# Token mixers in a one-core layer kernel: order of GpSimd's work, rests around small transfers, and how partial sums of a modulation are added

## The chip, the cores and the metric

One core of a Trainium2 chip runs one program: one inference step of a hybrid layer, 512 prompt frames and 64 sample frames, model width 2048, float32 in and out. The metric is the device time of that execution in microseconds (us). Of several executions the median is taken. Beside the time there is a profile of one execution: for every engine (TensorE = PE with its weight loads PEld, VectorE = DVE, ScalarE = ACT, GpSimd = POOL, and SP, which here only issues transfers) each instruction's start, duration and what ended the wait before it.

## The reference, cut to what matters

```python
mod = silu(c) @ w_ada + b_ada                       # 6 vectors of 2048 from one conditioning vector
sh1, sc1, g1, sh2, sc2, g2 = split(mod, 6)
h = rmsnorm(x, norm1) * (1 + sc1) + sh1
proj = h @ w_in                                     # 7200 columns, split between two mixers
# GLA: 4 heads, S_t = diag(a_t) S_{t-1} + k_t v_t^T, o_t = S_t^T q_t
# GDN: 8 heads; q, k, v = silu(causal_dwconv(q|k|v, 4 taps)); q, k normalised per frame;
#      S_t = a_t (I - b_t k_t k_t^T) S_{t-1} + b_t k_t v_t^T, o_t = S_t^T q_t
#      per block: sol = triangular_solve(I + lower, rhs, unit_diagonal=True)
# both: o = rmsnorm_per_head(o) * silu(gate)
x = x + g1 * (concat(o_gla, o_gdn) @ w_out)
h = rmsnorm(x, norm2) * (1 + sc2) + sh2
x = x + g2 * conv_ffn(h)                            # conv gate, w_up 2048 x 11264, w_down 5632 x 2048
y = rmsnorm(x, final_norm)
```

Prompt and sample share the weights. Final states and convolution tails are returned too.

## The kernel before

The activations lie transposed (features on partitions, 576 frames along the free axis, in two halves of 288). Every float32 weight tile is split into a rounded high part and the rest (`split`, L598 to L600: transfer on SP, high part on ACT, low part on DVE), and each product is made of three matmuls (`mm6`, L512 and L514). The program runs in this order: a head (input transposed, modulation vectors 0 and 1, the first projections); the **mixer stage** (projections, all heads, first half of the output projection, about 240 to 1260 us of the span); second half of the output projection; the up projection (L1300 to L1302); the down projection and the last norm. The change touches only the mixer stage and its helpers.

In the mixer stage the projection gemms run k-tile by k-tile, and after each k-tile (six matmuls) `tick` is called. It advances two kinds of side work that is written as Python generators:

- *jobs*, one generator for each head (`gdn`, `gla`). `job_step` goes through the list of open jobs, oldest first, until one of them does a real step. A generator that yields `WAIT` lets the next job have the same tick; `rest(n)` yields `WAIT` n times.
- *ada*: modulation vectors 2 to 5, blocks 8 to 23 of 512 columns (`ada_block`). Eight transfers of `w_ada` per block (L764), then per step one DVE instruction (L772, 128x512) that adds a weighted row into the running sum `acc[s]`, s = 0 for prompt and 1 for sample. At the end of a block the 128 partial sums of each column are added by TensorE (L778): eight products, each with a 128x128 piece of `acc` as the stationary operand and one column of ones as the moving one; `put_mod` adds the bias. `ADA_RATE` steps are made per k-tile.

A planner places the recorded instructions: each engine's order follows the order of emission as a priority, but where an instruction's inputs come late by the planner's own cost estimates, a later one may be placed ahead of it. On the chip an engine then runs its list strictly in that order. All transfers are issued from SP's list, so a transfer that must wait holds back those behind it. `_Sooner` (`self.jv`, `self.ja`) gives the jobs' DVE and ACT instructions 80 places of priority. `issue_after(x)` adds an edge: what is recorded inside it comes after x on its engine.

A GDN head runs: decay masks (`affine_select` on POOL, L181, L182), transposes of k and q with sums of squares and `rsqrt` (DVE adds EPS, L137; POOL takes the power, L138); two sets of products (L216, L222); `inverse16`, which inverts the 16x16 diagonal blocks of the triangle on POOL: write to DRAM (L340), read back with one block per partition (L345), 14 iterations of two POOL instructions (L351, L352), a copy (L354), write and read back (L355, L358), spread to full width on DVE (L362); then levels 16, 32, 64 on TensorE (from L238); then, once v is there, four blocks of recurrence (L276 to L305); `rsqrt` of the output's squares, normalisation on ACT, transposes (L144), gate, and the output's transfer `o_put`. The next head's job is open while the one before it ends.

`gdn_conv` (L907 to L925) makes the four-tap convolution of one q, k or v tile: copies from PSUM on ACT and DVE (L914, L915), four small copies on POOL (L916 to L919), one product on ACT, three on DVE, the SiLU on ACT. `put_s` sends the 64 sample frames of a tile to DRAM (L900).

Of the kernel before, what the change touches and what calls it, by code (L numbers as in the profile page):

```python
# [16 lines left out]
P = 128  # L17
D = 2048
KD = 16
TP, TS = 512, 64  # L20
# [8 lines left out]

AHEAD, JOB_AHEAD = 80, 80  # L30

JOB_RATE, ADA_RATE = 1.0, 0.65


REST_D, REST_X, REST_T, REST_N, REST_G = 8, 16, 2, 2, 3
LATE = 3
N_EARLY = 4
N_EXTRA = 24
# [57 lines left out]
class Kern:  # L96
    def __init__(self, tc, ctx, i, o):
        self.tc, self.nc, self.ctx, self.i, self.o = tc, tc.nc, ctx, i, o
        self.n = 0
        self.cp = ctx.enter_context(tc.tile_pool(name="cp", bufs=1, side="left"))  # L100
        self.pg = ctx.enter_context(tc.tile_pool(name="pg", bufs=2, space=PSUM))
        self.c = {}
        self.jv, self.ja = _Sooner(tc, tc.nc.vector), _Sooner(tc, tc.nc.scalar)

    def load_consts(self, pool, names):
        nc = self.nc
# [19 lines left out]
        return self.m(tag).rearrange("p (b t) -> p b t", b=4)  # L126

    def small(self, w):
        return self.sp.tile([P, w], F32, tag=f"s{w}", name=self.name(f"s{w}"))

    def half(self):
        return self.sp.tile([P, P], F32, tag="sq", bufs=4, name=self.name("sq"))
# [2 lines left out]
    def rsqrt(self, out, src, n, parts=P):  # L135

        self.nc.vector.tensor_scalar_add(out[:parts, :n], src[:parts, :n], EPS)  # L137
        self.nc.gpsimd.tensor_tensor(out[:parts, :n], out[:parts, :n], self.mhalf[:parts, :n], op=ALU.pow)  # L138

    def transpose4(self, src4, n=4):  # L140

# [13 lines left out]
    def gdn(self, qF, kF, x, gain, hcols, gb_src, s0, s_out, o_put, last_level):  # L155
# [10 lines left out]
        nc, c = self.nc, self.c  # L166
# [14 lines left out]
        nc.gpsimd.affine_select(du, du, pattern=[[0, 4], [1, P]], compare_op=ALU.is_ge, fill=0.0, base=0, channel_multiplier=-1)  # L181
        nc.gpsimd.affine_select(dl, dl, pattern=[[0, 4], [-1, P]], compare_op=ALU.is_gt, fill=0.0, base=0, channel_multiplier=1)  # L182
        if pair:
            nc.gpsimd.memset(du[0:64, :, 64:P], 0.0)
# [4 lines left out]
        junk = self.half()  # L189
        kps = self.transpose4(kF)  # L190
        kT = self.m4()
        for b in range(4):
# [116 lines left out]
            nc.sync.dma_start(s_out, st)  # L309

        ss, rr = self.small(8), self.small(8)
        junk = self.half()
# [8 lines left out]
        while "gate" not in x:  # L321
            yield WAIT
        V.tensor_tensor(kF, kF, x["gate"](), op=ALU.mult)
        o_put(kF)

    def rest(self, n):
# [4 lines left out]
    def inverse16(self, a):  # L331

        nc, c, G = self.nc, self.c, self.nc.gpsimd
# [10 lines left out]
        G.memset(lane[:, 0, 0:256:17], 1.0)  # L347
        for i in range(1, 15):
            rest = slice(i + 1, 16)
            sh = [32, 15 - i, i]  # L350
            G.tensor_tensor(xt[:, rest, :i], xx[:, rest, i:i + 1].to_broadcast(sh), xx[:, i:i + 1, :i].to_broadcast(sh), op=ALU.mult)  # L351
            G.tensor_tensor(xx[:, rest, :i], xx[:, rest, :i], xt[:, rest, :i], op=ALU.add)  # L352
            yield WAIT
        G.tensor_copy(xt, xx.rearrange("p i j -> p j i"))  # L354
        nc.sync.dma_start(d1.rearrange("w q f -> q w f"), lane)  # L355
        cm = self.sp.tile([P, 2, 4, 16], F32, tag="cm", bufs=1, name=self.name("cm"))
        for w in range(2):
            nc.sync.dma_start(cm[:, w], d1[w].rearrange("(b n) (i j) -> (n i) b j", b=4, i=16))  # L358
        sh = [P, 4, 8, 16]
        t, u = self.m4(), self.m4()  # L360
        for w, x in enumerate((t, u)):
            nc.vector.tensor_tensor(x.rearrange("p b (n j) -> p b n j", n=8), cm[:, w].unsqueeze(2).to_broadcast(sh),  # L362
                                    c["bd16"].rearrange("p (n j) -> p n j", n=8).unsqueeze(1).to_broadcast(sh), op=ALU.mult)
        yield from self.rest(REST_X)
        return u, t

    def gla(self, nb, qF, kF, g, x, s0, s_out, o_put):
# [103 lines left out]
        for f in range(2):  # L471
            dst = (qd, kd3)[f]
            while f"gate{f}" not in x:
                yield WAIT
            V.tensor_tensor(dst, dst, x[f"gate{f}"](), op=ALU.mult)
            o_put(f, dst)


    def tick(self):
# [266 lines left out]
    def put_mod(self, mi, k0, m):  # L746
        self.nc.vector.tensor_tensor(
            self.mod[:, mi, k0:k0 + 4], m,
            self.vec("b_ada", mi * KD + k0, 4).unsqueeze(2).to_broadcast([P, 4, 2]), op=ALU.add)

    def scale_mod(self, out, mi, norm, k0, n=4):

# [4 lines left out]
    def ada_block(self, blk, acc, raw):  # L757

        nc = self.nc
        V, T = nc.vector, nc.tensor  # L760
        acc = [a() for a in acc]
        for k0 in range(0, KD, 2):
            w = raw().rearrange("p (k n) -> p k n", k=2)
            nc.sync.dma_start(w, self.i["w_ada"][0, k0 * P:(k0 + 2) * P, blk * 512:(blk + 1) * 512]  # L764
                              .rearrange("(k p) n -> p k n", p=P))
            for k in range(2):
                for s in range(2):
                    col = self.ct[:, s, k0 + k:k0 + k + 1]
                    if k0 + k == 0:
                        V.tensor_scalar_mul(acc[s], w[:, k], col)  # L770
                    else:
                        V.scalar_tensor_tensor(acc[s], w[:, k], col, acc[s], op0=ALU.mult, op1=ALU.add)  # L772
                    yield
        yield from self.rest(4)
        pc = self.bank()
        for j in range(4):
            for s in range(2):
                T.matmul(pc[:, 2 * j + s:2 * j + s + 1], acc[s][:, j * P:(j + 1) * P], self.c["ones"][:, 0:1],  # L778
                         start=True, stop=True)
# [116 lines left out]
    def put_s(self, name, col, write):  # L896

        t = self.sp.tile([P, TS], F32, tag="ts", bufs=4, name=self.name("ts"))
        write(t)
        self.nc.sync.dma_start(self.sd[name][:, col * TS:(col + 1) * TS], t)  # L900

    def get_s(self, name, w=512):

# [4 lines left out]
    def gdn_conv(self, ps, t, dst, name, h):  # L908

        nc = self.nc  # L910
        V, A = nc.vector, nc.scalar
        cb = self.ap.tile([P, 582], F32, tag="cb", bufs=1, name=self.name("cb"))
        acc = self.ap.tile([P, 582], F32, tag="ca", bufs=1, name=self.name("ca"))
        A.activation(cb[:, 3:515].rearrange("p (h t) -> p h t", h=2), ps[:, :, :HP], AF.Copy)  # L914
        V.tensor_copy(cb[:, 518:582].rearrange("p (h t) -> p h t", h=2), ps[:, :, HP:HT])  # L915
        nc.gpsimd.tensor_copy(cb[:, 0:3], self.zero3)  # L916
        nc.gpsimd.tensor_copy(cb[:, 515:518], self.vmap["st_conv"].rearrange("p (i t) -> p t i", i=3)[:, t])
        nc.gpsimd.tensor_copy(self.cs[:, 0, :, t], cb[:, 512:515])
        nc.gpsimd.tensor_copy(self.cs[:, 1, :, t], cb[:, 579:582])  # L919
# [4 lines left out]
        A.activation(dst, acc[:, 0:512], AF.Silu)  # L924
        self.put_s(name, h, lambda s: A.activation(s, acc[:, 515:579], AF.Silu))  # L925

# [12 lines left out]
    def gdn_heads(self):  # L939
# [19 lines left out]
        def vg(h, x):  # L959
# [5 lines left out]
            self.put_s("g", h, lambda t: A.activation(self.halves(t), ps[:, :, HP:HT], AF.Silu))  # L965
            x["gate"] = lambda: b4(gt)

        xs = [qk(0)]
        for h in range(8):
            if h < 7:  # L970
# [641 lines left out]
class _Sooner:  # L1612
# [5 lines left out]
    def __getattr__(self, name):  # L1618
        f = getattr(self.engine, name)

        def g(*a, **kw):
            with self.tc.high_priority(offset=JOB_AHEAD):
                return f(*a, **kw)
        return g


class _States:


# [55 lines left out]
```

## Time and profile before

| | before |
|---|---|
| median of 3 executions | 2979.81 us (2978.62 to 2980.59) |
| profiled execution, its own time | 2981.26 us |
| its span in the profile | 2979.5 us |
| granted TensorE clock, mean | 0.98 |
| TensorE matmul busy | 2863.4 us, 96% |
| VectorE busy | 2050.0 us, 69% |
| ScalarE busy | 1179.3 us, 40% |
| GpSimd busy | 338.0 us, 11% |
| transfers | 395.55 MB, mean 133 GB/s |

An engine's busy time is the union of its instructions. The granted clock is 1.00 at full speed. A row of the timeline gives start, duration, engine, line, operation, output and inputs, shapes, the number of merged instructions, and in brackets the idle time before and what ended it. In the waits view a row gives total idle us, number of waits, longest. A row of the windows view gives the stretch, its length, each engine's busy time and number of instructions, then the granted clock, the share of the transfer engines and GB/s.

### The profile page before, as it was taken

What the parts mean: (1) busy time and instruction counts of PE and PEld (TensorE: products, weight loads), DVE (VectorE), ACT (ScalarE), POOL (GpSimd) and SP (SyncE); (2) the same over time, 40 slices, a digit from 0 to 9 for tenths busy, and PEclk for the clock granted to TensorE, in tenths of its full rate; (3) what the DMA queues carried; (4) which work ended last, traced back from release to release, by engine and by line L of the source; (5) the groups of instructions that cost most, each with busy time, mean ns of one, the idle gap of its engine ahead of it and who ended that gap; (6) DMA issues with size and microseconds to landing.
All of it is one profiled execution on the core that took longest, in us unless ns stands there. A gap on an engine that the chain in (4) does not pass through costs nothing.

```text
span 2979.5 us, 52341 instructions
## 1 busy us (share of the span) xinstructions
PE 2863.4 (96%) x21060; PEld 2772.9 (93%) x21060; DVE 2050.0 (69%) x3234; ACT 1179.3 (40%) x2015; POOL 338.0 (11%) x609
## 2 busy tenths in 40 slices
PE   6998899999899999999999999999999999999998
PEld 3688888999889998999999999999999999999997
DVE  2366766667668867557888888888888865555555
ACT  4234444444445333245444444444444421222223
POOL 0004323333120000000011111111111100000000
PEclk8999999999999999999999999999999999999999
DMA  8864544444454446643333333333333473333221
GB/s 269 285 185 121 150 143 124 128 129 144 134 159 130 137 132 194 199 140 97 106 105 111 109 103 107 111 102 105 115 105 105 133 236 101 111 101 113 84 85 66
DMA packets 535446, 395.55 MB, mean 133 GB/s; under 512 B 59657, under 2 KB 465412, under 8 KB 535204
## 3 DMA queue, kind: packets, MB, share of 16 engines
q1 hardware_dynamic: 535204, 392.21, 44.0%
q8 instruction: 166, 2.72, 0.4%
q14 instruction: 76, 0.62, 0.1%
HBM read 356.47 MB, written 35.67 MB: 132 GB/s over the span
## 4 chain that ended last, share of the span: by engine, by line
PE 71%; DVE 3%; DMA 2%; POOL 1%; issue 1%; ACT 1%; SPq 0%; ACTq 0%; DVEq 0%; POOLq 0%
PE g L512 22%; PE bank L1301 11%; PE bank L1300 11%; PE bank L1302 11%; PE g L514 11%; DVE acc L772 1%; PE bank L405 1%; PE bank L144 1%; DMA xr<-in_w_ada_dram 1%; DMA xr<-in_x_prompt_dram 1%; PE bank L778 1%; DVE wl L600 0%; POOL m L352 0%; POOL m L351 0%; POOL s L138 0%
## 5 line engine op out<-in xcount | busy, mean ns | idle before, releaser
L1301 PE MATMUL bank<-slot,wh 128*128 128x290 f32 x2464 | 736.3, 299 | 0.0
L1300 PE MATMUL bank<-slot,wh 128*128 128x290 f32 x2464 | 734.0, 298 | 0.0
L1302 PE MATMUL bank<-slot,wl 128*128 128x290 f32 x2464 | 728.2, 296 | 0.0
L512 PE MATMUL g<-slot,wh 128*128 128x288 f32 x3168 | 551.7, 295 | 0.3 <-DVE slot L1070 0.3
L512 PE MATMUL g<-hh,wh 128*128 128x288 f32 x2048 | 473.1, 310 | 0.0
L1302 PEld LDWEIGHTS bank<-slot,wl 128*128 128x128 f32 x2464 | 470.8, 191 | 0.0
L1301 PEld LDWEIGHTS bank<-slot,wh 128*128 128x128 f32 x2464 | 469.8, 191 | 0.1
L512 PEld LDWEIGHTS g<-slot,wh 128*128 128x128 f32 x3168 | 465.8, 188 | 0.7 <-DVE slot L1070 0.5
L599 ACT ACTIVATE wh<-raw 128x1024 fp32r<-128x1024 f32 x215 | 227.5, 1059 | 601.9 <-PE g L512 572.1
L1300 PEld LDWEIGHTS bank<-slot,wh 128*128 128x128 f32 x2464 | 464.2, 188 | 0.1
L512 PE MATMUL g<-hl,wh 128*128 128x288 f32 x2048 | 461.6, 304 | 0.0
L514 PE MATMUL g<-hh,wl 128*128 128x288 f32 x2048 | 459.9, 303 | 1.6 <-DVE wl L600 1.6
L1070 DVE SCALAR_TENSOR_TENSOR slot<-g,mod,slot 128x512 f32<-128x512 f32 (+1 forms) x448 | 202.1, 492 | 284.2 <-PE g L514 283.2
L772 DVE SCALAR_TENSOR_TENSOR acc<-xr,ct,acc 128x512 f32<-128x512 f32 x480 | 340.5, 752 | 26.6 <-DMA xr<-in_w_ada_dram 26.0
L512 PEld LDWEIGHTS g<-hh,wh 128*128 128x128 f32 x2048 | 336.6, 193 | 12.1 <-issue 9.8
L514 PEld LDWEIGHTS g<-hh,wl 128*128 128x128 f32 x2048 | 338.6, 193 | 8.4 <-issue 5.9
L512 PEld LDWEIGHTS g<-hl,wh 128*128 128x128 f32 x2048 | 340.4, 193 | 4.4 <-issue 3.9
L514 PE MATMUL g<-slot,wl 128*128 128x288 f32 x1584 | 342.8, 295 | 0.0
L600 DVE TENSOR_TENSOR wl<-raw,wh 128x1024 fp32r<-128x1024 f32 x215 | 262.5, 1221 | 62.4 <-ACT wh L599 61.7
L1247 ACT ACTIVATE wh<-raw 128x1024 fp32r<-128x1024 f32 x176 | 186.0, 1057 | 221.9 <-PE bank L1301 185.6
L514 PEld LDWEIGHTS g<-slot,wl 128*128 128x128 f32 x1584 | 255.3, 188 | 0.0
L1248 DVE TENSOR_TENSOR wl<-raw,wh 128x1024 fp32r<-128x1024 f32 x176 | 215.4, 1224 | 54.3 <-ACT wh L1247 54.3
(354 smaller groups left out, 3160.9 us busy)
## 6 DMA issues: line engine op xcount, KB each, us to landing
raw<-in_w_up_dram SPq DMA_DIRECT2D x176, 512.0 KB
xr<-in_w_ada_dram SPq DMA_DIRECT2D x128, 512.0 KB
raw<-in_w_in_dram SPq DMA_DIRECT2D x100, 512.0 KB
raw<-in_w_down_dram SPq DMA_DIRECT2D x88, 512.0 KB
hraw<-in_w_ada_dram SPq DMA_DIRECT2D x64, 512.0 KB
raw<-in_w_out_dram SPq DMA_DIRECT2D x32, 512.0 KB
slot<-actd SPq DMA_DIRECT2D x44, 288.0 KB
actd<-v SPq DMA_DIRECT2D x44, 256.0 KB
```

Source lines behind the costliest of these rows:

```text
L144: self.nc.tensor.transpose(ps[:, b * P:(b + 1) * P], src4[:, b], self.c["ident"])
L512: T.matmul(ps[:, h if bank is None else bank, :n], wh, x[:, h, :n], start=f, stop=False)
L514: T.matmul(ps[:, h if bank is None else bank, :n], wl, ah[:, h, :n], start=False, stop=stop)
L599: nc.scalar.activation(hi[:, :n_], raw[:, :n_], AF.Copy)
L600: nc.vector.tensor_tensor(lo[:, :n_], raw[:, :n_], hi[:, :n_].bitcast(F32), op=ALU.subtract)
L772: V.scalar_tensor_tensor(acc[s], w[:, k], col, acc[s], op0=ALU.mult, op1=ALU.add)
L1070: self.nc.vector.scalar_tensor_tensor(x1[:, :, z], ps[:, :, c], gain[:, q:q + 1], x1[:, :, z], op0=ALU.mult, op1=ALU.add)
L1247: self.nc.scalar.activation(hi, src, AF.Copy)
L1248: self.nc.vector.tensor_tensor(lo, src, hi.bitcast(F32), op=ALU.subtract)
L1300: T.matmul(ps, wh[:, j], hi, start=(c < 3 and j == 0), stop=False, skip_group_check=True)
L1301: T.matmul(ps, wh[:, j], lo, start=False, stop=False, skip_group_check=True)
L1302: T.matmul(ps, wl[:, j], hi, start=False, stop=(j == NPAIR - 1), skip_group_check=True)
```

## The change

1. `_InTurn` wraps GpSimd as `self.pool`: each of its instructions gets an edge to the one emitted before it. `rsqrt`, the masks and `inverse16` use it, so GpSimd's list is the order of emission for them.
2. `rest` is split up. The two rests of `inverse16` (8 ahead of the iterations, 16 at its end) become 2 and 3 around the first transfers, 6 ahead of the iterations, 2, 3, 4 and 4 around the second transfers and the spreading; the sum with the 14 iterations is 38 k-tiles, as before. The rest ahead of the last transposes of a GDN head goes from 2 to 4, and 4 are new ahead of `o_put`.
3. Small tiles `small(w)` have 8 buffers instead of 2; results of squares that nobody reads go to one tile `scrap` and no longer to one of the four `sq` buffers.
4. `gdn_conv`: the four POOL copies are gone. The zeros are written once, into a tile that stays; the state's columns are copied by DVE, and both output tails by one DVE copy after the convolution.
5. `put_s` issues its transfer from ACT's list (except for `ag`, which stays on SP).
6. `ada_block`: the partial sums are added with ones as the stationary operand in four products, each 32 output rows wide (row groups 0, 32, 64, 96 of one bank), 256 moving columns; ACT copies the 128x256 result, two rests, two transposes, and two `put_mod` of two columns each.
7. `ADA_RATE` goes from 0.65 to 0.72 steps per k-tile.

```diff
-JOB_RATE, ADA_RATE = 1.0, 0.65
-REST_D, REST_X, REST_T, REST_N, REST_G = 8, 16, 2, 2, 3
+JOB_RATE, ADA_RATE = 1.0, 0.72
+REST_S, REST_L, REST_D, REST_X, REST_U, REST_T, REST_N, REST_O, REST_G = 2, 3, 6, 4, 4, 2, 4, 4, 3
...
     def small(self, w):
-        return self.sp.tile([P, w], F32, tag=f"s{w}", name=self.name(f"s{w}"))
+        return self.sp.tile([P, w], F32, tag=f"s{w}", bufs=8, name=self.name(f"s{w}"))
+    def junk(self):
+        if not self.scrap:
+            self.scrap.append(self.kp.tile([P, P], F32, name="scrap"))
+        return self.scrap[0]
...
-        self.nc.gpsimd.tensor_tensor(out[:parts, :n], out[:parts, :n], self.mhalf[:parts, :n], op=ALU.pow)
+        self.pool.tensor_tensor(out[:parts, :n], out[:parts, :n], self.mhalf[:parts, :n], op=ALU.pow)
...
         V.tensor_tensor(kF, kF, x["gate"](), op=ALU.mult)
+        yield from self.rest(REST_O)
         o_put(kF)
...
+        yield from self.rest(REST_S)
         nc.sync.dma_start(d0[:P * pitch].rearrange("(p f) -> p f", p=P), a.rearrange("p b t -> p (b t)"))
+        yield from self.rest(REST_L)
...
         G.tensor_copy(xt, xx.rearrange("p i j -> p j i"))
+        yield from self.rest(REST_S)
         nc.sync.dma_start(d1.rearrange("w q f -> q w f"), lane)
+        yield from self.rest(REST_L)
...
+        yield from self.rest(REST_X)
         t, u = self.m4(), self.m4()
...
-        yield from self.rest(REST_X)
+        yield from self.rest(REST_U)
...
         yield from self.rest(4)
-        pc = self.bank()
-        for j in range(4):
-            for s in range(2):
-                T.matmul(pc[:, 2 * j + s:2 * j + s + 1], acc[s][:, j * P:(j + 1) * P], self.c["ones"][:, 0:1],
-                         start=True, stop=True)
-        self.put_mod(blk // 4, 4 * (blk % 4), pc[:, :8].rearrange("p (j s) -> p j s", s=2))
+        ps = self.bank()
+        for s in range(2):
+            for h in range(2):
+                r = 64 * s + 32 * h
+                T.matmul(ps[r:r + 32, :256], self.c["ones"][:, :32], acc[s][:, h * 256:(h + 1) * 256], start=True, stop=True)
+        rows = self.sp.tile([P, 256], F32, tag="qc", bufs=3, name=self.name("rows"))
+        self.nc.scalar.activation(rows, ps[:, :256], AF.Copy)
+        yield from self.rest(2)
+        pc = self.transpose4(rows.rearrange("p (b t) -> p b t", b=2), 2)
+        for h in range(2):
+            self.put_mod(blk // 4, 4 * (blk % 4) + 2 * h, pc.rearrange("p b (s c) -> p b s c", s=2)[:, :, :, 32 * h], 2)
...
-        self.nc.sync.dma_start(self.sd[name][:, col * TS:(col + 1) * TS], t)
+        (self.nc.sync if name == "ag" else self.nc.scalar).dma_start(self.sd[name][:, col * TS:(col + 1) * TS], t)
...
-        cb = self.ap.tile([P, 582], F32, tag="cb", bufs=1, name=self.name("cb"))
+        cb = self.conv_in
...
-        nc.gpsimd.tensor_copy(cb[:, 0:3], self.zero3)
-        nc.gpsimd.tensor_copy(cb[:, 515:518], self.vmap["st_conv"].rearrange("p (i t) -> p t i", i=3)[:, t])
-        nc.gpsimd.tensor_copy(self.cs[:, 0, :, t], cb[:, 512:515])
-        nc.gpsimd.tensor_copy(self.cs[:, 1, :, t], cb[:, 579:582])
+        V.tensor_copy(cb[:, 515:518], self.vmap["st_conv"].rearrange("p (i t) -> p t i", i=3)[:, t])
...
+        V.tensor_copy(self.cs[:, :, :, t], cb[:, 512:646].rearrange("p (s c) -> p s c", s=2)[:, :, 0:3])
...
+class _InTurn:
+    def __init__(self, tc, engine):
+        self.tc, self.engine, self.last = tc, engine, None
+    def __getattr__(self, name):
+        f = getattr(self.engine, name)
+        def g(*a, **kw):
+            with self.tc.issue_after(self.last) if self.last is not None else nullcontext():
+                r = f(*a, **kw)
+            self.last = self.tc.nc.cur_bb.bb.instructions[-1]
+            return r
+        return g
```

More of the change, by code (lines that the diff above doesn't have):

```diff
@@ L101, in __init__ @@
         self.pg = ctx.enter_context(tc.tile_pool(name="pg", bufs=2, space=PSUM))
-        self.c = {}
+        self.c, self.scrap = {}, []
         self.jv, self.ja = _Sooner(tc, tc.nc.vector), _Sooner(tc, tc.nc.scalar)
+        self.pool = _InTurn(tc, tc.nc.gpsimd)
     def load_consts(self, pool, names):
@@ L180, in gdn @@
         A.activation(du, du, AF.Exp, scale=-1.0)
-        nc.gpsimd.affine_select(du, du, pattern=[[0, 4], [1, P]], compare_op=ALU.is_ge, fill=0.0, base=0, channel_multiplier=-1)
-        nc.gpsimd.affine_select(dl, dl, pattern=[[0, 4], [-1, P]], compare_op=ALU.is_gt, fill=0.0, base=0, channel_multiplier=1)
+        self.pool.affine_select(du, du, pattern=[[0, 4], [1, P]], compare_op=ALU.is_ge, fill=0.0, base=0, channel_multiplier=-1)
+        self.pool.affine_select(dl, dl, pattern=[[0, 4], [-1, P]], compare_op=ALU.is_gt, fill=0.0, base=0, channel_multiplier=1)
         if pair:
-            nc.gpsimd.memset(du[0:64, :, 64:P], 0.0)
+            self.pool.memset(du[0:64, :, 64:P], 0.0)
         A.activation(gb, gb, AF.Exp)
         ss, kt = self.small(8), self.sp.tile([P, 4, 4], F32, tag="kt", bufs=3, name=self.name("kt"))
-        junk = self.half()
+        junk = self.junk()
         kps = self.transpose4(kF)
@@ L311, in gdn @@
         ss, rr = self.small(8), self.small(8)
-        junk = self.half()
+        junk = self.junk()
         for b in range(4):
@@ L331, in inverse16 @@
     def inverse16(self, a):
-        nc, c, G = self.nc, self.c, self.nc.gpsimd
+        nc, c, G = self.nc, self.c, self.pool
         pitch = 4 * P
@@ L475, in gla @@
             V.tensor_tensor(dst, dst, x[f"gate{f}"](), op=ALU.mult)
-            o_put(f, dst)
+        yield from self.rest(REST_O)
+        for f in range(2):
+            o_put(f, (qd, kd3)[f])
     def tick(self):
@@ L744, in sum_early, with put_mod @@
             nc.sync.dma_start(self.halves(self.sd[name][:, h * TS:(h + 1) * TS]), acc[:, :, HP:])
-    def put_mod(self, mi, k0, m):
+    def put_mod(self, mi, k0, m, n=4):
         self.nc.vector.tensor_tensor(
-            self.mod[:, mi, k0:k0 + 4], m,
-            self.vec("b_ada", mi * KD + k0, 4).unsqueeze(2).to_broadcast([P, 4, 2]), op=ALU.add)
+            self.mod[:, mi, k0:k0 + n], m,
+            self.vec("b_ada", mi * KD + k0, n).unsqueeze(2).to_broadcast([P, n, 2]), op=ALU.add)
     def scale_mod(self, out, mi, norm, k0, n=4):
@@ L966, in vg @@
             x["gate"] = lambda: b4(gt)
+        self.conv_in = self.ap.tile([P, 646], F32, name="conv_in")
+        nc.vector.tensor_copy(self.conv_in[:, 0:3], self.zero3)
         xs = [qk(0)]
```

## The prediction, made before the changed kernel was run

> **What bounds the kernel now.** I read the windows first, then the waits of PE, then the timeline around each long wait. The windows of the mixer stage (us; then PE, PEld, DVE, ACT, POOL busy, granted clock, transfer share, GB/s):
>
> ```profile
> 240.00:800.00 560.00, 508.58 (x3744) 491.73 (x3743) 360.48 (x610) 247.30 (x616) 178.67 (x359) 0.95 0.47 134
> 800.00:1150.00 350.00, 340.75 (x2480) 323.60 (x2479) 264.89 (x523) 147.64 (x310) 26.15 (x46) 0.98 0.47 138
> 1150.00:1260.00 110.00, 106.19 (x753) 101.42 (x752) 71.17 (x106) 32.87 (x54) 1.64 (x16) 0.97 0.77 219
> ```
>
> PE is the bound, with little idle: 51.4 + 9.3 + 3.8 = 64.5 us. But the clock is below 1.00 here: 0.05 x 560 + 0.02 x 350 + 0.03 x 110 = 38 us of full clock are missing. I put 8 of them into the idle time itself (an estimate), so 30 us of work are lost. All the change can give back here is about 95 us, and PE work that it removes. Where the idle time is (us, times, longest):
>
> ```profile
> PE bank L144 <- ACT m L1623: 28.1, 10, 9.1
> ...
> PE bank L276 <- DVE st L1623: 8.7, 1, 8.7
> PE bank L778 <- DVE m L1623: 8.3, 1, 8.3
> ...
> PE bank L144 <- ACT qkv L924: 5.9, 4, 1.9
> ```
>
> The first row is one place: the last transposes of each GDN head, which wait for the normalisation behind `rsqrt`. I followed the longest, around 305 to 313 us, through SP, DVE, POOL and PE:
>
> ```profile
> 293.39 0.38 SPq L598 DMA_DIRECT2D raw<-in_w_in_dram  x1
> 305.31 0.33 SPq L355 DMA_DIRECT2D d<-m  x1
> 309.62 0.75 DVE L772 SCALAR_TENSOR_TENSOR acc<-xr,ct,acc 128x512 f32<-128x512 f32 x1 [7.86 <-DMA xr<-in_w_ada_dram]
> 310.29 1.22 DVE L600 TENSOR_TENSOR wl<-raw,wh 128x1024 fp32r<-128x1024 f32 x1
> 311.43 0.16 DVE L137 TENSOR_SCALAR s<-s 128x4 f32<-128x4 f32 x1
> 304.69 0.59 POOL L354 COPY m<-m 32x256 f32<-32x256 f32 x1
> 311.67 1.44 POOL L138 TENSOR_TENSOR s<-s,mhalf 128x4 f32<-128x4 f32 x1 [6.39 <-DVE s L137]
> 313.60 0.47 PE L144 MATMUL bank<-consts,m 128*128 128x128 f32 x1 [9.14 <-ACT m L1623]
> ```
>
> Backwards: PE waited for the power, the power for DVE's add, DVE stood 7.86 us at the ada sum for a `w_ada` tile, and SP had issued nothing from 293.8 to 305.3, because L355 stood in its list ahead of its time and waited for POOL's copy: the inverse of the *next* head. Other heads have other roads to the same place:
>
> ```profile
> 376.67 0.27 DVE L137 TENSOR_SCALAR s<-s 128x4 f32<-128x4 f32 x1
> 380.18 0.59 POOL L354 COPY m<-m 32x256 f32<-32x256 f32 x1
> 380.75 1.01 POOL L138 TENSOR_TENSOR s<-s,mhalf 128x4 f32<-128x4 f32 x1
> 382.24 0.47 PE L144 MATMUL bank<-consts,m 128*128 128x128 f32 x1 [4.64 <-ACT m L1623]
> 456.21 0.69 DVE L362 TENSOR_TENSOR m<-cm,consts 128x512 f32<-128x512 f32 x1 [4.46 <-DMA cm<-d]
> 753.84 4.04 DMA xr<-in_w_ada_dram
> ```
>
> At 376.9 the add was done, but POOL finished the next head's inverse first (to 380.8). At 456 DVE stood at the spreading L362 for that inverse's transfer. The last row is from the chain of waits: ahead of the 8.7 us at L276 lies a late `w_ada` tile again. So the next head's inverse, placed too early in three lists, is one cause. And a wait costs more than itself; here PE works again since 313.6:
>
> ```profile
> 318.00:320.00 2.00, 2.00 (x11) 2.00 (x10) 2.00 (x5) 1.01 (x2) 1.27 (x2) 0.59 0.62 181
> 320.00:322.00 2.00, 2.00 (x18) 2.00 (x17) 2.00 (x4) 0.00 (x0) 0.00 (x0) 1.00 1.05 326
> ```
>
> 11 matmuls in 2 us instead of 18, until about 319.6: 6 us at half speed, 3 us lost.
>
> **The change part by part.**
>
> *GpSimd in order, and the rests.* I counted the generators in k-tiles. In the steady state head 2's iterations are emitted from k-tile 147 (now 150), after head 1's `rsqrt` at 141; the spreading moves from 161 to 173, the first level stays at 177. In the trace, though, the iterations ran before that `rsqrt`, since POOL had nothing else. With the edges they can't: SP's and DVE's long waits then fall behind the old head's end, where PE has only gemm work with weights buffered three deep. The transposes come 2 k-tiles later, 1.3 us (12 matmuls at the last row's 18 in 2 us). The chain after the last square is add, power 1.0 to 1.4, normalisation and queueing. I take 0.5 us of wait left per head: 28.1 becomes 4, a gain of 24 (ends: 10, if half the heads find DVE at another late transfer; 28). The 8.7 us at L276 have the same road, `w_ada` behind L355: gain 8.7 (ends 0 and 8.7). The 8.3 us at L778 belong to head 0, which has no head before it; only the convolution's POOL copies go from ahead of its inverse: gain 2 (ends 0 and 8.3).
>
> What it costs: the inverse starts later. For head 2:
>
> ```profile
> L347 POOL MEMSET m<- x1: 115/115/115, 365.1 to 365.1; 32x16 f32 x1
> L362 DVE TENSOR_TENSOR m<-cm,consts x2: 691/692/693, 385.4 to 387.0; 128x512 f32<-128x512 f32 x2
> L238 PE MATMUL bank<-m,m x24: 220/275/275, 410.2 to 489.1; 128*128 128x64 f32 x24
> ```
>
> It ran from 365.1 to 380.8, 15.7 us; from the copy's end to the second spreading's end at 387.7 took 6.9; the first level came at 410.2, 22.5 us of slack. Now it starts after the power, 376.9 + 1.3 = 378.2, and ends with the spreading at 378.2 + 15.7 + 6.9 = 400.8. The level comes at 410.2 less the 4.64 us of wait and about 3 us of half clock: 402.6. That leaves 1.8 us. I take 1 us of new wait and 1 us of clock per head, 12 us for six heads (ends 0 and the last rival's price).
>
> How long the inverse takes hangs on DVE. Two iterations' second instructions have the same shape, and the window shows DVE busy for 1.93 of 2 us at the slow one; at the fast one DVE stood idle (the 7.86 us above):
>
> ```profile
> 289.75 2.21 POOL L352 TENSOR_TENSOR m<-m 32x14 f32<-32x14 f32 x1
> ...
> 304.42 0.21 POOL L352 TENSOR_TENSOR m<-m 32x14 f32<-32x14 f32 x1
> 290.00:292.00 2.00, 2.00 (x17) 1.82 (x16) 1.93 (x4) 1.31 (x5) 1.96 (x1) 1.00 0.77 255
> ```
>
> So an iteration may cost up to ten times more beside a busy DVE. The Trainium skill has this as a rule (SBUF — State Buffer, "Who interferes with whom"): a DVE instruction with two SBUF inputs and a GpSimd instruction that reads SBUF exclude each other for their whole length. By that rule DVE, no longer held up, would stretch the inverse, and the sum would lose up to the last rival's price. The trace agrees with it as far as these rows go, 2.21 against 0.21 us.
>
> *Convolution and `put_s`.* POOL leaves the convolution's path, DVE gets two short copies in each of 24 (nearest row: the 0.27 us add, so 13 us in all, hidden under DVE's idle 36% of the stage). PE waits 5.9 us for convolutions: gain 3 (ends 0 and 5.9). 40 small transfers go from SP's list to ACT's:
>
> ```profile
> SPq L355 <- POOL m L354: 80.3, 8, 12.7
> SPq L900 <- ACT ts L925: 55.8, 19, 8.7
> ```
>
> SP's 55.8 us of waiting for convolutions at L900 goes. ACT writes these tiles itself, so it hardly waits; if it is held as SP is in the L355 row, 0.33 us each, that is 13 us under ACT's idle half. I cost it at nothing; were ACT full, up to 13. SP's 80.3 us at L355 may well stay; what changes is what PE needs at that time.
>
> *Small tiles and `scrap`.* Fewer waits for a free tile; none stands on PE's list above. Nothing (ends: a gain of 3, no loss, as nothing else moves).
>
> *Products of the modulation.* Now and then:
>
> ```profile
> 670.90 1.87 PEld L778 LDWEIGHTS bank<-consts,acc 128*128 128x128 f32 x16
> ...
> 107.98 1.06 PE L672 MATMUL bank<-hraw,cs 128*32 128x512 f32 x8
> 108.97 0.53 PE L512 MATMUL g<-hl,wh 128*128 128x288 f32 x2
> ...
> 248.33 0.85 PEld L144 LDWEIGHTS bank<-consts,qkv 128*128 128x128 f32 x8 [2.16 <-ACT qkv L924]
> ```
>
> A block takes 1.8 us at L778. The head's products at L672 have the new form, four row groups at once in two passes, but with 512 columns: 0.99 us to the next matmul. With 256 the streaming halves and the fixed part doesn't; I take 0.65, between 0.5 and 0.99, and 0.1 for the change-over. Two transposes are half of the last row, 0.43. Together 1.18 instead of 1.8, times 16: gain 10 (ends: nothing halves, 4; all halves and no change-over, 14; if ACT's copy comes late in every block, by the 5.9 / 4 = 1.5 us of the convolution's waits, a loss of 24 - 10 = 14).
>
> *Rate 0.72.* 16 blocks of 38 steps take 844 of 928 k-tiles (before 36 steps, 886). DVE gets 5% more ada work per k-tile and is done earlier. Nothing (ends: 3 either way, the size of the smaller waits).
>
> *Clock.* Of 30 us lost, 12 stay: 3.5 behind L778's wait and some five short waits of 1.7. Gain 18.
>
> Sum, against the profiled execution's 2981.3 (1.5 above the median of 2979.8): 24 + 8.7 + 2 + 3 + 10 + 18 - 12 = 54 gained: 2927.
>
> **The rivals.**
>
> *All waits go.* If the inverse is no later than its slack and the rests cover the chain, 15 us idle and 5 us of clock stay: 49 + 25 + 10 = 84, so 2897. For it: the 1.8 us of slack. Against it: the short waits have many roads.
>
> *The waits only move.* The planner still puts L355 and L362 too early, DVE and SP are held as long, and another PE instruction is the one to wait; only the products' 10 us come, less some wait for ACT's copy: 2974. For it: the 80.3 us at L355, which no part shortens. Against it: after the `rsqrt` PE has gemm work for 20 us.
>
> *The inverse ends last (slower).* Started behind `rsqrt` and stretched by a busy DVE, it makes the first level wait. With 12 us left out the gain is 66; with 3 us of half clock behind each wait, six heads lose it all when each level waits 66 / 6 - 3 = 8 us. At 10 us: 2981 - 66 + 78 = 2993. It needs an inverse of 26 us, where the trace has 15.7.
>
> **How the numbers follow.** Forecast 0.56, all waits go 0.19, waits only move 0.15, inverse last 0.10. A change under 0.2% (6 us) is about what this kernel's runs can't tell from none. Of "only move", 0.09 is faster and 0.06 the same: faster 0.84, same 0.06, slower 0.10. The range leaves out the slower case, the same case and a little at the fast end: 2885 to 2974. The likeliest case's own range is 2905 to 2950.
>
> **What would show it.** Right: in the waits of PE, L144 behind ACT's normalisation falls from 28.1 to under 8 and L276's 8.7 goes; every power of `rsqrt` runs before the next head's first iteration; the granted clock from 240 to 800 us is 0.97 or more; L778's 16-instruction bursts are gone, and the new ones with their transposes take about 1.1 us. Wrong: L238 waits for DVE's spreading in most heads (inverse last), or PE's idle time in the stage stays near 64 us at other lines (only moved). I would be wrong by less if the new transposes wait for ACT's copy in every block.

## The result, and the profile after

The changed kernel took 3011.89 us in the median (3009.20 to 3013.92), the kernel before 2980.20 us (2978.62 to 2984.36) on the same chip: a ratio of 1.0104 [1.0086, 1.0121]. It is 1.0% slower; 2927 had been forecast, with 2974 as the upper end. The profiled execution took 3013.92 us, its span is 3012.2.

The windows of the mixer stage after (us; then PE, PEld, DVE, ACT, POOL busy, granted clock, transfer share, GB/s):

```profile
240.00:800.00 560.00, 496.64 (x3603) 472.30 (x3602) 365.20 (x661) 244.53 (x615) 133.39 (x276) 0.93 0.46 130
800.00:1150.00 350.00, 327.95 (x2383) 309.67 (x2382) 256.09 (x507) 152.62 (x304) 26.54 (x43) 0.97 0.48 139
1150.00:1260.00 110.00, 101.20 (x707) 92.40 (x706) 75.26 (x124) 35.47 (x69) 4.91 (x19) 0.98 0.73 206
```

PE's idle time rose from 64.5 to 63.4 + 22.0 + 8.8 = 94.2 us, and the missing clock from 38 to 0.07 x 560 + 0.03 x 350 + 0.02 x 110 = 52 us, although the new products took PE work away. Where PE waited in these 1020 us, the seven largest rows (us, times, longest):

```profile
PE bank L252 <- DVE m L1649: 23.3, 3, 9.7
PE bank L252 <- DVE conv_in L939: 14.4, 4, 5.4
PE bank L246 <- DVE m L376: 10.7, 5, 5.1
PE bank L152 <- ACT qkv L947: 6.9, 5, 2.0
PE bank L246 <- DVE sq L1005: 6.7, 1, 6.7
PE bank L152 <- ACT m L1649: 6.6, 9, 1.3
PE bank L152 <- ACT rows L798: 4.8, 1, 4.8
```

Lines have moved: L144 is now L152, L238 is L246, L244 is L252, L276 is L284, L355 is L367, L362 is L376. What the change aimed at is gone: the transposes behind the normalisation wait 6.6 us instead of 28.1, and L276's 8.7 us have no row left. In their place stand the two products of a triangle's level, L246 and L252: 23.3 + 14.4 + 10.7 + 6.7 = 55 us (before, 2.0 + 1.7 at L244, nothing at L238). Of these, 6.45 us in front of 897.96 belong to the level of the sample frames. Their inverse stands behind no power: it begins at 863.97, when its own transfer has landed. So some 49 us are left for the prompt's heads, 8 per head over the six that wait.

How such a wait comes about is seen at head 2, the head of the prediction's working. First rows of GpSimd's list, then rows of all engines at the level; rows in between are left out:

```profile
351.85 1.46 POOL L1664 TENSOR_TENSOR rq<-rq,mhalf 128x4 f32<-128x4 f32 x1 [1.16 <-DVE rq L145]
376.54 1.01 POOL L1664 TENSOR_TENSOR s<-s,mhalf 128x4 f32<-128x4 f32 x1 [23.22 <-DVE s L145]
377.50 0.11 POOL L1664 MEMSET m<- 32x16 f32 x1
388.34 0.61 POOL L1664 COPY m<-m 32x256 f32<-32x256 f32 x1
402.29 0.68 DVE L376 TENSOR_TENSOR m<-cm,consts 128x512 f32<-128x512 f32 x1
403.24 1.00 PE L246 MATMUL bank<-m,m 128*128 128x64 f32 x8
406.08 4.19 DVE L788 SCALAR_TENSOR_TENSOR acc<-xr,ct,acc 128x512 f32<-128x512 f32 x6
410.19 0.41 DVE L1649 TENSOR_TENSOR m<-bank,consts 128x256 f32<-128x256 f32 x1
410.75 1.51 PE L252 MATMUL bank<-m,m 128*128 128x64 f32 x6 [5.40 <-DVE conv_in L939]
```

The first row is head 2's own power for `q`. The power of the old head runs at 376.54, and head 2's inverse begins the moment it ends. The spreading is done at 403.0 and the level starts at 403.2: no slack is left (22.5 us before). The second product then waits for DVE's masking of the first (410.19), which comes last in a list of DVE work that has piled up. The row names `conv_in` L939, but that is only the copy that DVE did next: the masking ends at 410.60 and PE starts 0.15 us later, the same distance as behind the masking at 577.89 below. The waits of 3.4 and 5.3 us in front of 332.25 and 495.37, under the same name, end 0.15 us behind a masking too, so L252's 14.4 us are waits for DVE's masking as well.

The longest of these waits, 9.68 us in front of 578.45, shows the road (rows of several engines, others left out):

```profile
538.59 0.12 POOL L1664 MEMSET m<- 32x16 f32 x1
...
554.01 0.61 POOL L1664 COPY m<-m 32x256 f32<-32x256 f32 x1
554.64 0.33 SPq L367 DMA_DIRECT2D d<-m  x1
560.59 2.74 DVE L788 SCALAR_TENSOR_TENSOR acc<-xr,ct,acc 128x512 f32<-128x512 f32 x4 [10.39 <-DMA xr<-in_w_ada_dram]
565.24 0.79 ACT L941 ACTIVATE ca<-conv_in,cols 128x579 f32<-128x579 f32 x1 [11.54 <-DVE conv_in L939]
565.52 0.57 SPq L181 DMA_DIRECT2D m<-gd  x1
570.86 0.40 ACT L1649 ACTIVATE m<-m,ncum 128x128 f32<-128x128 f32 x1 [3.89 <-DMA m<-gd]
576.56 0.58 ACT L938 ACTIVATE conv_in<-g 128x512 f32<-128x512 f32 x1
577.17 0.22 DVE L939 COPY conv_in<-g 128x64 f32<-128x64 f32 x1 [2.37 <-ACT conv_in L938]
577.89 0.41 DVE L1649 TENSOR_TENSOR m<-bank,consts 128x256 f32<-128x256 f32 x1
578.45 1.94 PE L252 MATMUL bank<-m,m 128*128 128x64 f32 x8 [9.68 <-DVE m L1649]
```

SP stands at the write of the inverse until GpSimd's copy is done (554.6). So a `w_ada` tile is late and DVE stands 10.39 us (to 560.6). So ACT stands 11.54 us for a convolution's copy (to 565.2), and SP issues the next head's mask rows at 565.5 only. So ACT is late with those masks, and the convolution's copy on ACT behind them (576.56), DVE's copy (577.17), the masking (577.89) and PE's product follow one another. Every engine is late by the inverse, and the level is the first thing that has no slack.

And a wait costs more than itself, as before. The same kernel in slices of 2 us from that product on:

```profile
578.40:580.40 2.00, 1.95 (x9) 1.98 (x10) 0.78 (x1) 0.87 (x1) 0.00 (x0) 0.50 0.00 1
...
582.40:584.40 2.00, 2.00 (x12) 2.00 (x12) 1.05 (x2) 1.31 (x2) 0.00 (x0) 0.58 0.24 48
584.40:586.40 2.00, 2.00 (x18) 2.00 (x18) 0.50 (x2) 1.13 (x3) 0.00 (x0) 1.00 0.72 214
```

Some 5.5 us at half clock, nearly 3 us lost behind 9.68 us of wait. The Trainium skill (TensorE: Matmul & The Clock Gate, "What's actually happening") says that the clock halves after an idle window of about 3.4 us and comes back after a busy one; this place agrees: the wait is longer than such a window, and the clock is back after between one and two. Another place does not: in the kernel before, a wait of only 2.04 us, up to 711.45, was followed by a granted clock of 0.50 from 713 to 715 as well.

### The profile page after: what moved, and what is told of

The parts are those of the page before. It is cut to its first block, busy times and chain, and to the rows that moved or that the text cites. A ratio compares the mean times of both kernels' runs of the same rounds, so it can differ in the third digit from the quotient of the medians.

```text
span 3012.2 us, 52046 instructions
## 1 busy us (share of the span) xinstructions
PE 2867.9 (95%) x20964; PEld 2759.5 (92%) x20964; DVE 2055.3 (68%) x3299; ACT 1187.4 (39%) x2033; POOL 290.7 (10%) x513
## 4 chain that ended last, share of the span: by engine, by line
PE 75%; issue 8%; DVE 6%; DMA 4%; POOL 4%; ACT 2%; SPq 0%; ACTq 0%; POOLq 0%; DVEq 0%
PE g L528 24%; PE g L530 12%; PE bank L1327 11%; PE bank L1326 11%; PE bank L1328 11%; POOL m L1664 2%; DVE acc L788 2%; PE bank L688 1%; PE bank L152 1%; DMA xr<-in_w_ada_dram 1%; PE bank L419 1%; DVE wl L616 1%; ACT m L1649 1%; PE bank L252 1%; PE g L661 1%
```

## The experiments

The theory after these readings: GpSimd's list in order of emission puts the next head's inverse behind the old head's power, the inverse begins 12 us later (head 2: 377.5 instead of 365.1), and the levels pay. The rivals: the edges cost by themselves; SP's stand at the inverse's write is the cause and not the late inverse; the new products or the rests cost. The runs were made on several chips, where the kernel before took 2984 to 2989 us in the median; so the ratio to that kernel on the same chip is what can be compared from run to run, and not the time.

**One part of the change taken away or done alone.** Without the edges, all else as changed:

```diff
-        self.pool = _InTurn(tc, tc.nc.gpsimd)
+        self.pool = tc.nc.gpsimd
```

> The changed kernel without the edges on GpSimd (all else as changed): the planner may again put the next head's iterations ahead of the old head's rsqrt. Theory START (the inverse starts only behind that rsqrt and the first level follows at once in PE's list): PE's waits at the first two products of a level (48 us in the changed kernel) fall under 10 us, the waits of the last transposes behind the normalisation come back above 6.6 us, and the time is 2985 or less. Rival LOAD (DVE is late because it has more to do: ada at 0.72 steps, the convolution's copies): the order of GpSimd changes little, the time stays at 3000 or more and the level waits above 30 us.

2979.19 us, 0.9972 [0.9960, 0.9983] of the kernel before. In PE's and SP's waits the picture of the kernel before returns, its normalisation waits too. The levels' waits are down to 12.4 us, a little over the 10 expected, and the 6.4 of them below are those of the sample frames, which do not hang on the edges:

```profile
PE bank L152 <- ACT m L1649: 29.4, 9, 8.5
...
PE bank L252 <- DVE m L1649: 6.4, 1, 6.4
...
SPq L367 <- POOL m L365: 71.4, 9, 11.9
```

The last row, SP's stand at the second write of the inverse, is 95.0 us in the changed kernel.

The kernel before with nothing but the edges (`self.pool` in order for all that GpSimd does in the heads):

> The kernel before with the edges on GpSimd alone (its convolution copies on GpSimd have no edges). START: each inverse begins behind the old head's rsqrt, PE waits 25 us or more at the levels, the time is 3000 or more. LOAD: no slower than before, 2980 or less, since the waits behind the normalisation (28 us) go.

3017.95 us, 1.0106 [1.0081, 1.0131], with the same waits at the level (L244 is L245 here), and the normalisation's down to 7.9:

```profile
PE bank L245 <- DVE cb L916: 30.2, 4, 9.6
PE bank L245 <- DVE m L1624: 11.2, 2, 9.0
```

The wait at the sample frames' level is 2.2 us in this run. So the edges alone carry the loss; everything else in the change together gives 0.28%.

**The level later.** The rest between the spreading and the level is 10 k-tiles instead of 4:

```diff
-REST_S, REST_L, REST_D, REST_X, REST_U, ... = 2, 3, 6, 4, 4, ...
+REST_S, REST_L, REST_D, REST_X, REST_U, ... = 2, 3, 6, 4, 10, ...
```

> The changed kernel with the rest behind the spreading at 10 instead of 4 k-tiles: the first level is emitted 6 k-tiles (about 6 us) later, in k-tiles in which the head waits for its v anyway. Theory NEAR (the level stands too near behind the spreading in PE's list; what ends late is the inverse itself): PE's waits at the first two products of a level fall from 48 us to under 20, the time to 2990 or less. Rival STAND (SP stands at POOL's copy and so w_ada tiles, the next head's mask rows and with them DVE and ACT come 10 us late, which the level meets): 6 us are not enough, waits of 25 us or more stay there, DVE's idle time for w_ada stays near 41 us, the time is 3000 or more.

3015.44 us, 1.0088 [1.0073, 1.0103]: not to be told from the changed kernel. The levels' waits fell below 20, to 11.7 at L252 and 5.0 at L246, as the first theory had it, but the time did not follow; others took their place:

```profile
PE bank L152 <- ACT qkv L947: 30.0, 5, 8.6
```

The wait has moved to the opening transposes of the next head, which now stand ahead of the level in PE's list. At 416.92, for example, they wait 7.84 us for that head's `k`, whose convolution DVE and ACT finish late, and the products of L230 and then the level follow at once. So it isn't only that one product comes too early: with DVE and ACT late, the next instruction of PE that needs them waits. With 12 k-tiles in place of 10 the program deadlocks, so there is no time for it.

**The inverse first.** With edges, but all its 14 steps emitted together right behind the triangle's products, so that in the order of emission they stand ahead of the old head's power; the rests keep their sum:

```diff
-REST_S, REST_L, REST_D, REST_X, REST_U, ... = 2, 3, 6, 4, 4, ...
+REST_S, REST_L, REST_D, REST_X, REST_U, ... = 0, 1, 1, 13, 4, ...
...
             G.tensor_tensor(xx[:, rest, :i], ..., op=ALU.add)
-            yield WAIT
...
-        yield from self.rest(REST_S)
+        yield from self.rest(16)
...
-        yield from self.rest(REST_L)
+        yield from self.rest(3)
```

> The changed kernel with GpSimd's edges, but all iterations of an inverse emitted in one k-tile, 2 k-tiles behind the triangle's products, so that in the order of emission they stand ahead of the old head's rsqrt; the sum of rests is kept. Both theories: the level waits go (under 10 us), the waits behind the normalisation come back (20 us or more), time 2970 to 2990. If the edges as such cost (whatever the order): 3000 or more.

2994.3 us, 1.0019 [1.0008, 1.0029]. The edges stayed, most of the loss went; the time is over the 2970 to 2990 expected, on a chip where the kernel before took 2989. PE's waits:

```profile
PE bank L152 <- ACT m L1648: 26.4, 8, 7.7
PE bank L284 <- DVE st L1648: 14.4, 3, 7.5
PE bank L252 <- DVE m L1648: 10.6, 3, 6.4
```

The normalisation and the states' product wait again, the levels little: the two orders are a choice between two places for the waiting, and the old place is the cheaper one. This version is still 0.5% slower than the one without edges (0.9972), and their intervals don't touch; what makes up that rest is not shown.

**SP's stand.** The second write of the inverse and the two reads back are issued from GpSimd's list, right behind the copy, so that SP doesn't stand for them:

```diff
-        nc.sync.dma_start(d1.rearrange("w q f -> q w f"), lane)
+        G.dma_start(d1.rearrange("w q f -> q w f"), lane)
...
-            nc.sync.dma_start(cm[:, w], ...)
+            G.dma_start(cm[:, w], ...)
```

> The changed kernel with the inverse's second write and its two reads back issued from GpSimd's list instead of SP's, so that SP never stands at POOL's copy (95 us in the changed kernel). STAND: DVE's idle time for w_ada falls from 41 us to under 20, the level waits from 48 to under 20, the time to 2985 or less. NEAR: the inverse ends no earlier, the level waits stay above 30 us, the time at 3000 or more.

3011.3 us, 1.0072 [1.0057, 1.0087], against 1.0104 of the changed kernel. DVE's waits for `w_ada` fell from 41.4 to 8.4 us, so that link of the chain was real; but the levels still wait, 54.8 us in all. DVE now stands at the spreading itself, for longer than before (43.7 in the changed kernel):

```profile
PE bank L252 <- DVE m L1649: 28.7, 5, 8.9
...
DVE m L376 <- DMA cm<-d: 77.4, 9, 11.1
...
DVE acc L788 <- DMA xr<-in_w_ada_dram: 8.4, 9, 3.3
```

SP's stand is one of two roads from the late inverse to a late DVE, not the cause. The same edit without the edges:

> The same transfers from GpSimd's list in the kernel without edges (2979 on the chip, 0.28% under before). STAND: 10 to 25 us less than that kernel, 2955 to 2970, as the waits behind the normalisation had SP's stand among their roads. NEAR: no difference beyond 5 us.

2979.7 us, 0.9964 [0.9954, 0.9975]: not to be told from the kernel without edges; its normalisation waits are 26.4.

**The inverse shorter.** With edges, but only 7 of the 14 steps are computed; the last 7 are left out, so the output is not the reference's:

```diff
-        for i in range(1, 15):
+        for i in range(1, 8):
```

> The changed kernel with its edges, but only 7 of the 14 steps of the 16 x 16 inverse are computed (the last 7 are left out, so the output is not the reference's). Order and rests stay as they are up to the shorter count of steps; GpSimd has half of its chain, so the inverse ends some 5 to 7 us earlier though it begins as late. Theory (the lateness of the inverse's end is what costs): SP's stand at the second write falls from 95 us to under 50, the waits at the levels from 55 to under 20, those behind the normalisation stay under 10, and the time is 2965 to 2980, ratio 0.997. Rival (it is the edges' order and not the lateness: other GpSimd instructions are held): 3005 to 3012 with the waits at the levels over 40. Rival (steps fewer means also k-tiles fewer between the masks and the level, the level comes as much earlier as the inverse): the level's slack stays at nothing and the time at 3005.

2966.4 us, 0.9934 [0.9913, 0.9955], against 1.0104 with all steps. Its waits of PE and SP, and the sum over the three windows:

```profile
PE bank L246 <- DVE m L376: 12.2, 4, 4.1
PE bank L252 <- DVE conv_in L939: 11.1, 3, 5.4
...
SPq L367 <- POOL m L1664: 66.4, 9, 9.4
...
sum 1020.00, PE 957.36 PEld 907.38 DVE 715.13 ACT 439.18 POOL 113.85; mean PE 319.12 PEld 302.46 DVE 238.38 ACT 146.39 POOL 37.95
```

Nothing but the length of the chain on GpSimd was changed, and with it 7 k-tiles of the distance to the level. The idle time fell by 94.2 - 62.6 = 31.6 us, the normalisation's waits stayed away (7.6), the levels' fell by half. The waits at the levels were expected under 20 and SP's stand under 50; both missed (25.9 and 66.4), presumably since the write and the level come nearer with the steps. The time lies in the range of 2965 to 2980, the ratio below the 0.997 expected. With the order and the edges kept, then, what the change loses hangs on when that chain ends. How much a shorter chain would gain without the edges was not run.

**The power off GpSimd.** If one instruction, the old head's power, makes the choice, then moving it ends the choice. No edges, and ACT computes this power:

```diff
-        self.rsqrt(rr, ss, 4)
+        A.activation(rr[:, :4], ss[:, :4], AF.Ln, bias=self.eps)
+        A.activation(rr[:, :4], rr[:, :4], AF.Exp, scale=-0.5)
```

> The changed kernel without the edges on GpSimd, and the power of the last normalisation of each GDN head computed on ACT (logarithm and exponential, two short instructions, with up to two table loads of 1.28 us) instead of DVE's add and GpSimd's power. So neither order of GpSimd's list is paid: the old head's normalisation does not stand behind the next head's inverse, and the inverse does not stand behind it. Theory (the two orders are a choice between two waits, 29.4 us at the normalisation or 55 us at the levels): both stay small, the normalisation's waits fall from 29.4 to under 10 us, levels near 10: 2955, ratio 0.989. Rival (the wait moves on: ACT's list with its table loads is late too): normalisation waits of 15 to 30 us, 2970 to 2985. Rival (the edges cost by themselves, not by what stands where): no difference to the run without edges, 2979.

2971.06 us, 0.9947 [0.9926, 0.9967]; expected was 0.989. Of its waits of PE:

```profile
PE bank L252 <- DVE conv_in L940: 10.3, 4, 6.4
...
PE bank L252 <- DVE m L1652: 6.3, 4, 5.1
...
PE bank L152 <- ACT m L1652: 5.1, 6, 1.3
```

Both waits are small at once (the levels' are 19.4 us with L246's 2.8), and the granted clock from 240 to 800 us is 0.97. And with the edges put back over this version:

> The changed kernel with its edges on GpSimd, and with the last power of each GDN head computed on ACT as in the run before this one; so the edges stay but the one instruction that held the next head's inverse is gone from GpSimd's list. Theory (the edges cost only because this one instruction is ahead of the inverse): as without edges and with the power on ACT, 2965 to 2978, ratio 0.993 to 0.997 of the kernel before; waits at the levels under 25 us. Rival (other instructions in GpSimd's list, the masks of the next head among them, hold the inverse too): 2990 to 3010, levels over 40 us, SP's stand at the second write over 90 us.

2972.84 us, 0.9956 [0.9939, 0.9972]. The edges cost nothing that can be told, once this power isn't in that list. From GpSimd's list there, head 2's power for `q` and the start of its inverse, to be read beside the changed kernel's 351.85 and 377.50 above:

```profile
343.93 1.47 POOL L1667 TENSOR_TENSOR rq<-rq,mhalf 128x4 f32<-128x4 f32 x1 [1.16 <-DVE rq L145]
363.42 0.11 POOL L1667 MEMSET m<- 32x16 f32 x1 [18.03 <-PE bank L291]
```

Head 2's inverse starts 14 us earlier. From the end of its own power for `q` it is 18.0 us instead of 24.2, so 6 of the 14 are the hold at this head, and 8 are lateness that the head had brought along from the ones before. The row puts the release down to PE's L291, a product of the old head; the transfers that bring the triangle's blocks (L357) were issued at 357.85 to 359.94, and in the run without edges the same instruction is put down to them. In either case no power holds it. That settles which of GpSimd's orders costs: power before inverse. The last run joins the power on ACT, without edges, with the transfers issued from GpSimd's list:

> The fastest version so far (no edges, last power on ACT) with the second write of the inverse and its two reads issued from GpSimd's list instead of SP's. SP stood 70 us at that write there. If SP's stand is what is left of the waits for the modulation's weights on DVE (41 us) and so for the levels (10.3 and 6.3 us): 2955 to 2963, ratio 0.992. If these waits lie under PE's work, as they did when the same edit was made without the edges: 2968 to 2974, no difference that can be told.

2965.97 us, 0.9930 [0.9916, 0.9945]: the fastest version that computes all of the reference, and faster than both kernels. It lies between what the two expectations had, and against the version with SP's issues the intervals overlap, so this step by itself is not shown.

**The products.** On the kernel before, the new products alone, at the old rate of 0.65:

> The kernel before with the new sum of the modulation's partial sums alone (four products side by side, ACT's copy, two transposes). The prediction's term says 10 us less, 2970; both theories have that. If the transposes wait for ACT's copy in most blocks: 2980 to 2995.

2994.5 us, 1.0027 [1.0015, 1.0038], but not a price of the products: 16 blocks of 38 steps at 0.65 need 935 k-tiles of the 928, so the modulation's last product ran at 1289 us, after the stage. So the products with the rate of 0.72, still on the kernel before:

> The kernel before with the new products of the modulation and the rate of 0.72, nothing else of the change. In the run with the products alone at 0.65 the modulation ended 40 us late and a stretch behind it ran uncovered, so that run gave no clean price. Theory (products as I costed them, the gain of 10 us is real and the rate costs nothing): 2970, a ratio of 0.9965, with the last modulation row near 1250 us. Rival (the new products bring nothing, since ACT's copy of the rows comes late or the wait at the next line takes it): 2978 to 2982. Rival (they cost): above 2986.

2985.4 us, 0.9998 [0.9986, 1.0010]. A row of PE's waits there, the groups of instructions of the products and their transposes, and the sum of its windows:

```profile
PE bank L244 <- DVE m L1629: 8.7, 2, 7.9
...
L779 PE MATMUL bank<-acc,consts 128*32 128x256 f32 x128 | 10.2, 391 | 0.0
...
L144 PE MATMUL bank<-consts,rows 128*128 128x128 f32 x32 | 6.7, 294 | 13.6 <-ACT m L1629 9.1 <-ACT rows L781 4.5
...
sum 1020.00, PE 934.25 PEld 884.42 DVE 698.86 ACT 435.79 POOL 213.00; mean PE 311.42 PEld 294.81 DVE 232.95 ACT 145.26 POOL 71.00
```

and the group of the old products in the kernel before:

```profile
L778 PE MATMUL bank<-consts,acc 128*128 128x1 f32 x256 | 31.4, 253 | 8.3 <-DVE m L1623 8.3
```

PE's busy time for this falls by 31.4 - 16.9 = 14.5 us, more than the 10 promised. Its idle time is 1020 - 934.25 = 85.8 us instead of 64.5, and nothing reaches the time. One new wait can be named: 7.9 us at the sample frames' level, in front of 881.54, where the kernel before has 1.7. It is 8.2 in the run with the products alone and 6.4 in the version without edges, so it goes with the products. The waits behind the normalisation are longer too (34.5 us instead of 28.1). Whether PE merely comes earlier to waits that other engines end, or those engines are later, is not shown.

## Why the prediction was wrong, point by point

The step that failed is the last term of the sum, the late inverse at 12 us, and the sentence that it rests on: that SP's and DVE's long waits "then fall behind the old head's end, where PE has only gemm work". With it went the term for the clock, 18 us that were to come back.

- **When the inverse runs: right.** Forecast for head 2: start 378.2, spread by 400.8, level at 402.6. Measured: 377.5, 403.0, 403.2.
- **What no slack costs: wrong by size.** From 1.8 us of slack I took 1 us of wait and 1 us of clock per head. I had priced only the transfer from the spreading to the first product. Behind that product comes the masking on DVE and a second product, and DVE's and ACT's lists were themselves late by the same inverse. Measured: 49 us at the heads' levels, 8 per head over six, instead of 6 us in all, and 6.4 more at the samples', which came with the products. The gemm work covered the hold of SP and DVE, and used up the time that the level had.
- **The normalisation's waits: right.** 28.1 to 6.6, a gain of 21.5 for a forecast of 24. L276's 8.7 us went too. L778's 8.3 went, but 4.8 came at the new transposes: 3.5 for 2.
- **Convolution: wrong, small.** PE's waits for it are 6.9 us instead of 5.9; I had forecast a gain of 3.
- **Products: the PE work right, its worth wrong.** 10 us were forecast; PE's work fell by 14.5, and the time, in the run with these products and the rate alone, by 0.02% [-0.10, 0.14], so at most 4 us. Work taken off the engine that bounds the kernel was worth nothing that can be told: in the same windows the engine's idle time grew by 21 us.
- **Clock: wrong sign.** The granted clock from 240 to 800 us is 0.93, where I asked for 0.97 or more; 52 us are missing instead of 38, where 18 were to come back. There are more long waits: 10 of PE's over 3.4 us from 240 to 1260 us, 58 us together, instead of 6 with 40 us.
- **The sum.** In the stage: 29.7 us more idle time, 14 of clock, 14 less of PE work, about 30 of the 32.7 us by which the span grew.
- **The rivals.** "The inverse ends last" had the right place and the size of the wait, 8 to 10 us per level, at 0.10. Its time was too short all the same: at 8 us it has 2981, and 3012 was measured, since it kept the gains of the clock and of the products, which did not come. Its mechanism, an inverse stretched to 26 us by a busy DVE, was not what happened: head 2's took from 377.5 to 388.95, 11.5 us, the one that began at 538.59 16.0, and the longest of the nine 16.4 (17.3 in the kernel before). The Trainium skill's rule that stood for it (SBUF — State Buffer, "Who interferes with whom") is not contradicted, but no run here shows its price. "The waits only move" was the other half of the truth. I argued against it with 20 us of gemm work, and that counted one engine's cover for a delay that went through three lists.

## What to carry to other kernels

Where two chains share one in-order engine, ask for each order which chain ends later and what each of its followers has left, counting every engine that a late transfer holds and not only the consumer. If both orders cost, try to take the smaller chain off that engine: two short ACT instructions per head in place of one on DVE and one on GpSimd made both waits small here. A slack near zero in the forecast became a wait in the trace, and PE work saved between waits on other engines was no time saved.

## What the hardware showed that I had not expected

The logarithm and exponential for 128x4 took 0.30 and 0.21 us on ACT in the version without edges, and ACT made 22 more table loads of 1.28 us each in that program (71, the changed kernel 49). Behind head 0's last square, for example, one load stands ahead of the logarithm (306.36) and another between the two (307.97), so that the pair takes 3.1 us with its loads. Yet the waits behind the normalisation were shorter, 5.1 us, than with GpSimd's power in front of the next head's inverse, 6.6 us.
